# Seven products of half operands for the second layer's down projection, with the operands' sums made beside the gate and up products

## The chip, the cores and the metric

The kernel runs on one core of one Trainium2 chip. The metric is device time in microseconds (us) of one execution. A profiled execution gives the trace from which everything below is read; its times are counted from the first instruction of the span.

## The reference, cut to what matters

The program is one inference step of a two-layer trunk: an RWKV-7 layer, then a layer of band attention, each followed by a SwiGLU feed-forward part. There are 1,152 token columns (1,024 of a prompt, 128 of eight samples), 1,024 features, and 2,816 hidden features. All of it is fp32. The part at issue is the second layer's feed-forward part:

```python
def swiglu(h, w_gate, w_up, w_down):
    return (jax.nn.silu(h @ w_gate) * (h @ w_up)) @ w_down
...
        h = modulate(rms_norm(x, p['norm_ffn'][l]), sh_f, sc_f)
        x = x + gt_f[:, None, :] * swiglu(h, p['w_gate'][l], p['w_up'][l], p['w_down'][l])
```

## The kernel before, in words

Activations lie with features on the 128 partitions and tokens along the columns. The columns are held in two parts, c = 0 (512 tokens) and c = 1 (640 tokens). Every fp32 product on TensorE is made of three passes: `split` (L271) writes a rounded copy `hi` with ACT and the remainder `lo` with VectorE (DVE), and `mm3` (L275) multiplies hi by hi, hi by lo and lo by hi. So each weight tile that comes from DRAM costs one ACT and one DVE instruction, and each 128-row step of a product costs three matmuls.

**Gate and up.** `ffn` (L1392) calls `gate_up` (L1350) 22 times in the second layer, once for each f of 128 hidden features; the first of them is made in two halves. This stage already uses a Strassen-Winograd scheme: the two weight matrices against the two halves of the features, on the two halves of each token part, take seven products instead of eight. Each product is 12 matmuls of 256 columns (part 0) and 12 of 320 (part 1) into one of three PSUM tiles, S, S and PT. The products come in the order 0, 1, 2, 4, 5, 6, 3, and the names t1, s0, s1, t5, u2, u3 below are the sums into which they go. POOL (GpSimd) makes three sums of 576 columns for every f (L1369), here called ADD1 and ADD2 (into s1) and ADD3 (into t5); DVE then multiplies s1 by t5 (L1383) and s0 by u3 (L1385), and the two results go by DMA to the DRAM tensor `sd`. `strassen_weights` (L1322) loads four 128x512 weight tiles on the SP queue into the five buffers `rq`, and POOL makes four sums of them (L1340 to L1343). The weights' hi and lo lie in 16 buffers `w`, eight pairs, so weights are made about one f ahead. The token operands B fill 14 buffers of each of the two pools h0 and h1.

**Down.** The second half of `ffn` goes over 11 pairs p of hidden tiles. For each pair `begin` loads the pair of activations from `sd`, splits them, and loads four weight tiles of 128x512. For each of 8 output tiles n, part 0 takes six matmuls of 512 columns, and part 1 takes two times six of 320. DVE adds the result to the accumulators in SBUF (L1436), and at the end the residual goes in (L1170) and the result goes to `y`. Eight plain products of half operands would be the same number of columns.

**Order.** The program is written in one go and put in order by a scheduler before it runs; each engine, and the SP queue that issues nearly all DMAs, then runs its own list strictly in order. An instruction that waits holds up all that stands behind it in its list. `order` rows below show such lists.

Of the kernel before, what the change touches and what calls it, by code (L numbers as in the profile page):

```python
# [58 lines left out]
def _solver_identity():  # L59
    return np.ascontiguousarray(np.broadcast_to(np.eye(16, dtype=np.float32).reshape(1, 256), (128, 256)))  # L60
# [7 lines left out]
def _fm(v):  # L68
    return np.ascontiguousarray(np.asarray(v, np.float32).reshape(-1, 128).T)


def _tiles(w):
    k, n = w.shape
    return np.ascontiguousarray(w.reshape(k // 128, 128, n // 128, 128).transpose(2, 1, 0, 3)).reshape(n // 128, 128, k)


def prep(i):
    i = {k: np.asarray(v) for k, v in i.items()}
    d = {}
# [66 lines left out]
class Trunk:  # L146
# [372 lines left out]
    def spill(self, n, b, f, t):  # L519
        self.nc.sync.dma_start(self.sp[b][n][:, :, f, :], t.rearrange("p (w t) -> p w t", t=128))  # L520
# [753 lines left out]
    def cols(self, c):  # L1274
        return slice(512 * c, 512 + 640 * c)
# [71 lines left out]
        yield put(a21)  # L1347
        yield put(a22)

    def gate_up(self, sd, B, W, cs):  # L1350

        nc = self.nc
        dve = nc.vector
        gp = nc.gpsimd
        n0, n1 = 256 * cs[0], 576 if cs[-1] else 256
        new = (lambda: self.halfraw()[:, :n1]) if n1 == 256 else (lambda: self.ev("t")[:, n0:n1])

        def product(i):
            hi, lo = next(W)
            t = self.wide()[:, 256:832]  # L1360
            for c in cs:
                z = (t[:, 0:256], t[:, 256:576])[c]
                for k in range(4):
                    s = slice(k * 128, (k + 1) * 128)
                    self.mm3(z, hi[:, s], lo[:, s], B[c][i][0][:, k], B[c][i][1][:, k], k == 0, k == 3)
            return t[:, n0:n1]

        def add(eng, out, x, y):
            eng.tensor_tensor(out, x, y, ALU.add)  # L1369
# [6 lines left out]
        nc.scalar.activation(t5, product(4), AF.Copy)  # L1376
# [6 lines left out]
        dve.tensor_tensor(s1, s1, t5, ALU.mult)  # L1383
        add(dve, u3, product(3), u3)
        dve.tensor_tensor(s0, s0, u3, ALU.mult)  # L1385
        for h, s in enumerate((s0, s1)):
            for c in cs:
                o, n = 256 * c - n0, (256, 320)[c]
                t0 = 512 * c + n * h
                nc.sync.dma_start(sd[:, t0:t0 + n], s[:, o:o + n])  # L1390

    def ffn(self, l, B, W, part1, xsrc, dst, done):  # L1392

        nc = self.nc
        sd = [self.dp.tile([128, 2, 1152], F32, name=f"sd{l}_{p}") for p in range(11)]
        self.gate_up(sd[0][:, 0], B, iter(W), (0,))
        for _ in part1:
            pass
        self.gate_up(sd[0][:, 0], B, iter(W), (1,))
        for f in range(1, 22):  # L1400
            self.gate_up(sd[f // 2][:, f % 2], B, self.strassen_weights(l, f, nc.vector if f == 1 else None), (0, 1))
        self.ada = self.ada_steps(range(12, 28), "acc", 1) if l == 0 else iter(())
# [14 lines left out]
        for p, c in [(p, c) for p in range(9) for c in range(2)] + [(9, 1), (10, 1), (9, 0), (10, 0)]:  # L1417
# [6 lines left out]
                for n in range(8):  # L1424
                    ns = slice(n % 4 * 128, (n % 4 + 1) * 128)
                    d, parts = self.pz(c)
                    for z, o, m in parts:
                        for i in range(2):
                            wh, wl = W[p][i][n // 4]
                            hi, lo = (act[p, c][h][:, i, o:o + m] for h in range(2))  # L1430
# [12 lines left out]
                    if p == 7:  # L1443
                        x = self.ev("xin")[:, :y.shape[-1]]
# [541 lines left out]
```

## Time and profile before

| | |
|---|---|
| three runs | 3810.66 us median (3802.68 to 3817.41) |
| profiled execution, its own time | 3804.49 us |
| its span, first to last instruction | 3802.7 us |
| PE, DVE, ACT, POOL busy over the span | 92%, 60%, 41%, 16% |
| granted TensorE clock, mean | 0.940 |
| second layer's gate and up, from about 3050 us on at full clock | ends at 3520.35 us |
| second layer's down projection | 3520.35 us to the end |

In a timeline row the columns are the start, the length, the engine (SPq is the SP queue), the line, the operation, the tiles written and read, the sizes, and how many such instructions were put together; in brackets stands the idle time ahead of it and what ended it. Where rows put several matmuls together, their pace is read from the distance of two starts, since ends of matmuls are modelled and overlap. In a source row the three numbers are the shortest, the median and the longest duration in ns.

### The profile page before, as it was taken

To read this page: it belongs to the slowest core of one execution; us is meant where nothing else is said; L and a number is where in the kernel's file an instruction comes from. 1 tells how busy PE (TensorE), PEld (TensorE's weight loads), DVE (VectorE), ACT (ScalarE), POOL (GpSimd) and SP (SyncE) were. 2 spreads that over 40 slices of the span, in tenths; PEclk is the share of its full clock that TensorE was granted. 3 is DMA by queue.
4 is the path that set the end of the run, shared out by engine and by line. 5 is a ranking of instruction groups with operands and counts; after the bars stand their busy time and mean duration, and the time that the engine had idled before them with its cause. 6 is when DMAs were issued, how large, how long until landed. Compare 5 with 4: busy or idle time off the path is not lost.

```text
span 3802.7 us, 72100 instructions
## 1 busy us (share of the span) xinstructions
PE 3506.1 (92%) x28550; PEld 3098.0 (81%) x28550; DVE 2263.6 (60%) x4396; ACT 1573.8 (41%) x3006; POOL 591.6 (16%) x497
## 2 busy tenths in 40 slices
PE   5889989989999799999999899789889799999999
PEld 4777778777667699999888879667677799999898
DVE  4666667765445854554457742666565755545667
ACT  5545546544223533333311452556554533333310
POOL 0000000000011154453000100000000255444000
PEclk9887899899699899999999999899899899999999
DMA  5876776776665322224654122554565322222521
GB/s 212 236 216 170 207 220 184 201 203 201 192 197 176 113 84 76 76 73 157 221 177 172 64 71 92 153 151 155 152 203 178 120 78 71 76 75 96 171 86 66
DMA packets 426995, 554.01 MB, mean 146 GB/s; under 512 B 128385, under 2 KB 292737, under 8 KB 422177
## 3 DMA queue, kind: packets, MB, share of 16 engines
q1 hardware_dynamic: 351344, 450.68, 36.9%
q0 software_dynamic: 22224, 80.36, 6.9%
q10 hardware_dynamic: 53088, 18.36, 2.1%
q8 instruction: 225, 3.69, 0.4%
q14 instruction: 114, 0.93, 0.1%
HBM read 415.85 MB, written 133.40 MB: 144 GB/s over the span
## 4 chain that ended last, share of the span: by engine, by line
PE 69%; DMA 11%; DVE 10%; issue 4%; ACT 4%; SPq 1%; ACTq 0%; POOL 0%; DVEq 0%; POOLq 0%
PE S L143 32%; PE PT L143 15%; PE acc L143 12%; PE st L143 3%; PE O L143 2%; PE G L143 1%; DVE h L273 1%; PE aux L143 1%; PE PT L1811 1%; PE Y L143 1%; DMA TT<-Z 1%; DMA h<-out_kT 1%; DVE wlo L273 1%; DMA raw<-in_rw_o 1%; DMA h<-in_wo 1%
## 5 line engine op out<-in xcount | busy, mean ns | idle before, releaser
L143 PE MATMUL S<-h,w 128*128 128x320 f32 (+1 forms) x4944 | 689.7, 298 | 12.3 <-ACT h L272 4.8
L143 PEld LDWEIGHTS S<-h,w 128*128 128x128 f32 x4944 | 671.8, 191 | 18.4 <-ACT h L272 5.6
L143 PE MATMUL S<-h,wh 128*128 128x320 f32 (+1 forms) x2844 | 529.8, 338 | 15.9 <-DVE h L1170 6.8
L143 PE MATMUL acc<-mx,whi 128*128 128x384 f32 x1728 | 508.5, 372 | 32.7 <-ACT whi L272 13.0
L143 PEld LDWEIGHTS S<-h,wh 128*128 128x128 f32 x2844 | 456.1, 189 | 70.8 <-issue 12.3
L272 ACT ACTIVATE w<-rq 128x512 fp32r<-128x512 f32 x308 | 192.6, 629 | 515.1 <-PE S L143 201.1
L143 PEld LDWEIGHTS acc<-mx,whi 128*128 128x128 f32 x1728 | 337.6, 204 | 63.3 <-ACT whi L272 16.9
L273 DVE TENSOR_TENSOR w<-rq,w 128x512 fp32r<-128x512 f32 x308 | 267.8, 872 | 199.8 <-ACT w L272 199.0
L143 PE MATMUL PT<-h,w 128*128 128x320 f32 (+1 forms) x2448 | 347.6, 297 | 10.2 <-ACT h L272 4.7
L143 PEld LDWEIGHTS PT<-h,w 128*128 128x128 f32 x2448 | 332.1, 190 | 12.2 <-ACT h L272 5.1
L143 PE MATMUL acc<-mx,wlo 128*128 128x384 f32 x864 | 316.1, 366 | 8.3 <-DVE wlo L273 8.3
L1369 POOL TENSOR_TENSOR t<-t,t 128x576 f32<-128x576 f32 (+1 forms) x132 | 226.5, 1717 | 442.2 <-ACT t L1376 320.1
L143 PE MATMUL PT<-h,wh 128*128 128x320 f32 (+1 forms) x1428 | 284.2, 342 | 8.2 <-ACT h L1558 2.3
L143 PEld LDWEIGHTS PT<-h,wh 128*128 128x128 f32 x1428 | 231.7, 188 | 38.5 <-issue 5.0
L143 PEld LDWEIGHTS acc<-mx,wlo 128*128 128x128 f32 x864 | 175.0, 203 | 20.6 <-DVE wlo L273 12.9
L273 DVE TENSOR_TENSOR wlo<-raw,whi 128x1024 fp32r<-128x1024 f32 x114 | 139.1, 1221 | 84.9 <-ACT whi L272 83.8
L272 ACT ACTIVATE wh<-rq 128x512 fp32r<-128x512 f32 x124 | 74.8, 625 | 245.1 <-PE S L143 161.4
L273 DVE TENSOR_TENSOR h<-h,h 128x1024 fp32r<-128x1024 f32 (+4 forms) x112 | 122.3, 1106 | 88.3 <-ACT h L272 72.1
L272 ACT ACTIVATE whi<-raw 128x1024 fp32r<-128x1024 f32 x114 | 119.6, 1053 | 129.0 <-PE acc L143 62.6
L272 ACT ACTIVATE h<-h 128x1024 fp32r<-128x1024 f32 (+4 forms) x112 | 103.5, 935 | 159.8 <-DMA h<-sd 111.1
L1369 DVE TENSOR_TENSOR t<-S,t 128x576 f32<-128x576 f32 (+1 forms) x116 | 86.4, 744 | 122.7 <-PE S L143 122.7
L1436 DVE TENSOR_TENSOR h<-h,S 128x640 f32<-128x640 f32 (+1 forms) x150 | 111.9, 750 | 78.9 <-PE S L143 78.7
(444 smaller groups left out, 5625.0 us busy)
## 6 DMA issues: line engine op xcount, KB each, us to landing
h<-in_wada SPq DMA_DIRECT2D x64, 512.0 KB, 6.3
rq<-in_wg SPq DMA_DIRECT2D x88, 256.0 KB, 2.6
rq<-in_wu SPq DMA_DIRECT2D x88, 256.0 KB, 2.6
rq<-in_wd SPq DMA_DIRECT2D x88, 256.0 KB, 3.1
raw<-in_wada POOLq DMA_DIRECT2D x32, 512.0 KB, 5.0
kc<-in_ck SPq DMA_DIRECT2D x16, 1024.0 KB, 5.1
vc<-in_cv SPq DMA_DIRECT2D x16, 1024.0 KB, 6.0
sd<-t SPq DMA_DIRECT2D x88, 160.0 KB, 1.9
```

The source lines that it names most:

```text
L143: return nc.tensor.matmul(out, lhsT, rhs, start=start, stop=stop)
L272: self.nc.scalar.activation(hi, x, AF.Copy)
L273: self.nc.vector.tensor_tensor(lo, x, hi, ALU.subtract)
L1369: eng.tensor_tensor(out, x, y, ALU.add)
L1436: nc.vector.tensor_tensor(y, y, d, ALU.add)
L1811: nc.tensor.transpose(pt[:, j * 128:(j + 1) * 128], P[:, j * 128:(j + 1) * 128], self.C("ident"))
```

## The change

The second layer's down projection becomes one Strassen-Winograd scheme over the whole product: `w_down` is cut into halves of the 2,816 hidden features (even and odd tiles f) and of the 1,024 outputs, the tokens of each part into two halves. There are seven products, in the order 0, 1, 2, 4, 5, 6, 3; each has 4 output tiles m, 11 steps k of 128 hidden features, and parts of 256 and 320 columns. Both operands of the seven products need sums.

- *Activation sums* (`down_open`). After an even f its two results are held and one is stored; after an odd f DVE makes four sums of 128x576 from both pairs (t6, e1, e0, t3), and six tiles go to DRAM tensors `Bd`. The old stores to `sd` go away in this layer.
- *Weight sums* (`down_sums`). `wd1` is laid out anew by the host. It is handled in 64 groups of 88 columns: a DMA loads a 128x4x88 tile, POOL makes four sums of 128x88 in place, a DMA stores the tile to the DRAM tensors `Ws`. There is one buffer for it (`bufs=1`), so a group's load waits for the store of the group before. Three groups are written behind each f.
- *The products* (`down`). For each product, operand tiles are loaded from `Bd` and split, the weights of one m (1,408 columns) come in three loads from `Ws` or `wd1`; three products' results are held in SBUF, and DVE combines them (L1582) before the residual.

```diff
-        d[f"wd{l}"] = i["w_down"][l].reshape(22, 128, 1024)
+    d["wd0"] = i["w_down"][0].reshape(22, 128, 1024)
+    d["wd1"] = i["w_down"][1].reshape(11, 2, 128, 2, 4, 128).transpose(2, 3, 1, 4, 0, 5).reshape(128, 4, 5632)
...
         for f in range(1, 22):
-            self.gate_up(sd[f // 2][:, f % 2], B, self.strassen_weights(l, f, nc.vector if f == 1 else None), (0, 1))
+            self.gate_up(spill(f), B, self.strassen_weights(l, f, nc.vector if f == 1 else None), (0, 1))
+            if l:
+                for g in range(3 * f - 3, 64 if f == 21 else 3 * f):
+                    self.down_sums(g)
+        if l:
+            return self.down(48 * l + 40, xsrc, dst)
...
+        def odd(p):
+            def f(s0, s1, cs):
...
+                e0, e1 = held
+                t6, t3 = (self.ev("t")[:, 0:576] for _ in range(2))
+                put(p, 2, s1)
+                nc.vector.tensor_tensor(t6, s1, e1, ALU.subtract)
+                put(p, 6, t6)
+                nc.vector.tensor_tensor(e1, e1, e0, ALU.subtract)
+                put(p, 4, e1)
+                nc.vector.tensor_tensor(e0, e0, t6, ALU.add)
+                put(p, 5, e0)
+                put(p, 1, s0)
+                nc.vector.tensor_tensor(t3, s0, e0, ALU.subtract)
+                put(p, 3, t3)
...
+    def down_sums(self, g):
+
+        nc, gp = self.nc, self.nc.gpsimd
+        m, j = divmod(g, 16)
+        q = self.wq.tile([128, 4, 88], F32, tag="ws", name=self.nm("ws"), bufs=1)
+        nc.sync.dma_start(q, self.a["wd1"][:, :, g * 88:(g + 1) * 88])
+        gp.tensor_tensor(q[:, 3], q[:, 2], q[:, 3], ALU.add)
+        gp.tensor_tensor(q[:, 2], q[:, 0], q[:, 2], ALU.subtract)
+        gp.tensor_tensor(q[:, 0], q[:, 3], q[:, 0], ALU.subtract)
+        gp.tensor_tensor(q[:, 1], q[:, 1], q[:, 0], ALU.subtract)
+        nc.sync.dma_start(self.Ws[m][:, :, j * 88:(j + 1) * 88], q)
+
+    def down(self, gate, xsrc, dst):
...
+        for i in (0, 1, 2, 4, 5, 6, 3):
+            X = operand(i)
+            if i in (0, 2, 4):
+                hold(i)
+            for m in range(4):
+                W = weights(i, m)
+                d = self.wide()[:, 256:832]
+                for c in range(2):
+                    for n, (j, k) in enumerate(ks):
+                        s = slice(k * 128, (k + 1) * 128)
+                        hi, lo = (X[c][j][h][:, k] for h in range(2))
+                        self.mm3(d[:, part[c]], W[j][0][:, s], W[j][1][:, s], hi, lo, n == 0, n == 10)
...
+                if i == 1:
+                    add(oc, z, t[0])
+                    result(0, 0, m, o)
...
+                elif i == 3:
+                    add(oc, z, t[0])
+                    result(1, 0, m, o)
```

Line numbers below L133 are one higher in the changed kernel as far as L1350, so POOL's sums of L1369 and L1340 to L1343 are L1370 and L1341 to L1344 there.

POOL's list in the middle of the second layer's gate and up stage, before the change: the three sums of one f, then the four sums of weights for a later f, then ADD1 of the next f.

```order
L1369 TENSOR_TENSOR t_35036<-t_35036,t_35037 128x576 [waits DMAHW2_49,DMAHW1_49,Activation_49]
L1369 TENSOR_TENSOR t_35036<-t_35036,t_35038 128x576 [waits DVE_49,Pool_49]
L1369 TENSOR_TENSOR t_35037<-t_35037,t_35039 128x576 [waits DMAHW7_49,DMAHW0_49,DVE_49]
L1340 TENSOR_TENSOR rq_35589<-rq_35524,rq_35526 128x512 [waits DMAHW6_49,DMAHW5_49,DVE_49]
L1341 TENSOR_TENSOR rq_35524<-rq_35520,rq_35524 128x512 [waits DMAHW3_49,Pool_49]
L1342 TENSOR_TENSOR rq_35520<-rq_35589,rq_35520 128x512 [waits DVE_49,Pool_49]
L1343 TENSOR_TENSOR rq_35522<-rq_35522,rq_35520 128x512 [waits DMAHW4_49,DVE_49,Pool_49]
L1369 TENSOR_TENSOR t_35276<-t_35276,t_35277 128x576 [waits DMAHW2_49,DMAHW1_49,Activation_49]
```

The same place after the change, from ADD3 of one f on; a DMAHW wait of L1516 is that for its group's load.

```order
L1370 TENSOR_TENSOR t_33768<-t_33768,t_33770 128x576 [waits DVE_49]
L1341 TENSOR_TENSOR rq_34367<-rq_34302,rq_34304 128x512 [waits DMAHW6_49,DMAHW4_49,DVE_49]
L1342 TENSOR_TENSOR rq_34302<-rq_34298,rq_34302 128x512 [waits DMAHW0_49,Pool_49]
L1343 TENSOR_TENSOR rq_34298<-rq_34367,rq_34298 128x512 [waits DVE_49,Pool_49]
L1516 TENSOR_TENSOR ws_34547<-ws_34547 128x88 [waits DMAHW7_49,DMAHW0_49]
L1517 TENSOR_TENSOR ws_34547<-ws_34547 128x88 [waits Pool_49]
L1344 TENSOR_TENSOR rq_34300<-rq_34300,rq_34298 128x512 [waits DMAHW2_49,DVE_49]
L1518 TENSOR_TENSOR ws_34547<-ws_34547 128x88 [waits Pool_49]
L1519 TENSOR_TENSOR ws_34547<-ws_34547 128x88 [waits Pool_49]
L1516 TENSOR_TENSOR ws_34554<-ws_34554 128x88 [waits DMAHW7_49,DMAHW1_49,Pool_49]
L1517 TENSOR_TENSOR ws_34554<-ws_34554 128x88 [waits Pool_49]
L1518 TENSOR_TENSOR ws_34554<-ws_34554 128x88 [waits Pool_49]
```

Each f now has three groups in POOL's list, in this repeating order: ADD1, ADD2, group A, ADD3, three sums of weights, half of group B, the fourth sum of weights, the rest of B, group C, and then ADD1 of the next f. Groups B and C stand next to each other.

The SP queue's list at the same place before: four loads of weights, then the four stores of one f's two results.

```order
L1335 DMA rq_34080<-in_wg 128x512 [waits DMAHW3_49,DVE_49]
L1335 DMA rq_34082<-in_wg 128x512 [waits DMAHW4_49,DVE_49]
L1335 DMA rq_34084<-in_wu 128x512 [waits DMAHW5_49,DVE_49]
L1335 DMA rq_34086<-in_wu 128x512 [waits DMAHW6_49,DVE_49]
L1390 DMA sd_3_31786<-t_33596 128x256 [waits DMAHW7_49,DVE_49]
L1390 DMA sd_3_31786<-t_33596 128x320 [waits DMAHW0_49]
L1390 DMA sd_3_31786<-t_33595 128x256 [waits DMAHW1_49,DVE_49]
L1390 DMA sd_3_31786<-t_33595 128x320 [waits DMAHW2_49]
```

After, in an odd f, from the load of group B (L1515) to the store of group C (L1520):

```order
L1515 DMA ws_34547<-in_wd 128x4x88 [waits DMAHW7_49,DMAHW0_49]
L1476 DMA bd_0_31800<-t_33767 128x576 [waits DVE_49]
L1476 DMA bd_0_31812<-t_34001 128x576 [waits DMAHW2_49,DVE_49]
L1476 DMA bd_0_31797<-t_33766 128x576 [waits DVE_49]
L1476 DMA bd_0_31806<-t_33509 128x576 [waits DMAHW4_49,DVE_49]
L1476 DMA bd_0_31809<-t_33508 128x576 [waits DVE_49]
L1476 DMA bd_0_31803<-t_34002 128x576 [waits DMAHW6_49,DVE_49]
L1520 DMA ws_31816<-ws_34547 512x1x88 [waits DMAHW0_49,Pool_49]
L1336 DMA rq_34567<-in_wg 128x512 [waits DVE_49]
L1515 DMA ws_34554<-in_wd 128x4x88 [waits DMAHW7_49,DMAHW1_49]
L1336 DMA rq_34569<-in_wg 128x512 [waits DMAHW2_49,DVE_49]
L1520 DMA ws_31816<-ws_34554 512x1x88 [waits DMAHW3_49,DMAHW1_49,Pool_49]
```

The six stores of the activation sums, which wait for DVE, stand between a group's load and its store, and the loads of weights stand among the groups' loads and stores.

More of the change, by code (lines that the diff above doesn't have):

```diff
@@ L1348, in strassen_weights, with gate_up @@
         yield put(a22)
-    def gate_up(self, sd, B, W, cs):
+    def gate_up(self, put, B, W, cs):
         nc = self.nc
@@ L1385, in gate_up @@
         dve.tensor_tensor(s0, s0, u3, ALU.mult)
[L1386 to L1390, printed above, removed]
+        put(s0, s1, cs)
     def ffn(self, l, B, W, part1, xsrc, dst, done):
@@ L1395, in ffn, with spill, put @@
         sd = [self.dp.tile([128, 2, 1152], F32, name=f"sd{l}_{p}") for p in range(11)]
-        self.gate_up(sd[0][:, 0], B, iter(W), (0,))
+        def spill(f):
+            def put(s0, s1, cs):
+                for h, s in enumerate((s0, s1)):
+                    for c in cs:
+                        o, n = 256 * (c - cs[0]), (256, 320)[c]
+                        t0 = 512 * c + n * h
+                        nc.sync.dma_start(sd[f // 2][:, f % 2, t0:t0 + n], s[:, o:o + n])
+            return put
+        if l:
+            spill = self.down_open()
+        self.gate_up(spill(0), B, iter(W), (0,))
         for _ in part1:
             pass
-        self.gate_up(sd[0][:, 0], B, iter(W), (1,))
+        self.gate_up(spill(0), B, iter(W), (1,))
         for f in range(1, 22):
-            self.gate_up(sd[f // 2][:, f % 2], B, self.strassen_weights(l, f, nc.vector if f == 1 else None), (0, 1))
+            self.gate_up(spill(f), B, self.strassen_weights(l, f, nc.vector if f == 1 else None), (0, 1))
+            if l:
+                for g in range(3 * f - 3, 64 if f == 21 else 3 * f):
+                    self.down_sums(g)
+        if l:
+            return self.down(48 * l + 40, xsrc, dst)
         self.ada = self.ada_steps(range(12, 28), "acc", 1) if l == 0 else iter(())
@@ L1452, in ffn, with down_open, put, first @@
         return end
+    def down_open(self):
+        nc = self.nc
+        self.Bd = [[self.dp.tile([128, n, 576], F32, name=f"bd{i}_{j}") for j, n in enumerate((4, 4, 3))] for i in range(7)]
+        self.Ws = [self.dp.tile([128, 4, 1408], F32, name=f"ws{m}") for m in range(4)]
+        b12 = self.dp.tile([128, 576], F32, name="b12")
+        held = []
+        def put(p, i, t):
+            nc.sync.dma_start(self.Bd[i][p // 4][:, p % 4], t)
+        def first(s0, s1, cs):
+            cr = slice(256, 576) if cs[0] else slice(0, 256)
+            nc.sync.dma_start(self.Bd[0][0][:, 0, cr], s0)
+            nc.sync.dma_start(b12[:, cr], s1)
+        def even(p):
+            def f(s0, s1, cs):
+                put(p, 0, s0)
+                held[:] = s0, s1
+            return f
+        def odd(p):
+            def f(s0, s1, cs):
+                if p == 0:
+                    held[:] = (self.ev("t")[:, 0:576] for _ in range(2))
+                    nc.sync.dma_start(held[0], self.Bd[0][0][:, 0])
+                    nc.sync.dma_start(held[1], b12)
+                e0, e1 = held
[10 more added lines that the diff above has]
+                put(p, 3, t3)
+            return f
+        return lambda f: first if f == 0 else (odd if f % 2 else even)(f // 2)
@@ new lines, in down, with operand, weights, hold @@
+    def down(self, gate, xsrc, dst):
+        nc = self.nc
+        ks = [(j, k) for j, n in enumerate((4, 4, 3)) for k in range(n)]
+        part = (slice(0, 256), slice(256, 576))
+        T = {}
+        def operand(i):
+            X = {0: [], 1: []}
+            for c in range(2):
+                n = (256, 320)[c]
+                for j, nk in enumerate((4, 4, 3)):
+                    raw, hi, lo = (self.slot(c, dt)[:, :nk * n].rearrange("p (k t) -> p k t", k=nk) for dt in (F32, F32R, F32R))
+                    nc.sync.dma_start(raw, self.Bd[i][j][:, :, part[c]])
+                    self.split(hi, lo, raw)
+                    X[c].append((hi, lo))
+            return X
+        def weights(i, m):
+            src = {0: 0, 1: 1, 3: 3}.get(i)
+            src = self.Ws[m][:, {5: 0, 2: 1, 6: 2, 4: 3}[i]] if src is None else self.a["wd1"][:, src, m * 1408:(m + 1) * 1408]
+            W = []
+            for o, n in ((0, 512), (512, 512), (1024, 384)):
+                raw = self.halfraw()[:, :n]
+                nc.sync.dma_start(raw, src[:, o:o + n])
+                W.append([self.wq.tile([128, 512], F32R, tag="w", name=self.nm("w"), bufs=16) for _ in range(2)])
+                self.split(W[-1][0][:, :n], W[-1][1][:, :n], raw)
+            return W
+        def hold(n):
+            T[n] = [self.slot(c)[:, :4 * (256, 320)[c]].rearrange("p (m t) -> p m t", m=4) for c in range(2)]
+        def result(h, t, m, o):
+            f = 4 * h + m
+            at = [slice(512 * c + (256, 320)[c] * t, 512 * c + (256, 320)[c] * (t + 1)) for c in range(2)]
+            x = self.ev("xin")[:, 0:576]
+            for c in range(2):
+                nc.sync.dma_start(x[:, part[c]], xsrc[:, f, at[c]])
+            self.residual(448 if t else 576, f, gate, o, x, o)
+            for c in range(2):
+                nc.sync.dma_start(dst[:, f, at[c]], o[:, part[c]])
+        for i in (0, 1, 2, 4, 5, 6, 3):
[5 more added lines that the diff above has]
+                d = self.wide()[:, 256:832]
+                for c in range(2):
+                    for n, (j, k) in enumerate(ks):
+                        s = slice(k * 128, (k + 1) * 128)
+                        hi, lo = (X[c][j][h][:, k] for h in range(2))
+                        self.mm3(d[:, part[c]], W[j][0][:, s], W[j][1][:, s], hi, lo, n == 0, n == 10)
+                z = [d[:, part[c]] for c in range(2)]
+                t = {n: [T[n][c][:, m] for c in range(2)] for n in T}
+                o = None if i in (0, 2, 4) else self.ev("o")[:, 0:576]
+                def add(out, a, b):
+                    for c in range(2):
+                        nc.vector.tensor_tensor(out[c], a[c], b[c], ALU.add)
+                if i in (0, 2, 4):
+                    for c in range(2):
+                        nc.scalar.activation(t[i][c], z[c], AF.Copy)
+                oc = None if o is None else [o[:, part[c]] for c in range(2)]
+                if i == 1:
+                    add(oc, z, t[0])
+                    result(0, 0, m, o)
+                elif i == 4:
+                    add(t[2], t[2], t[4])
+                elif i == 5:
+                    add(t[0], z, t[0])
+                    add(oc, t[2], t[0])
+                    result(0, 1, m, o)
+                elif i == 6:
+                    add(t[0], z, t[0])
+                    add(oc, t[4], t[0])
+                    result(1, 1, m, o)
+                elif i == 3:
+                    add(oc, z, t[0])
+                    result(1, 0, m, o)
```

## The prediction

> **What bounds the kernel now.** I read the page's busy line and slices first, then the busy time by stage, then the timelines of PE and POOL in the second layer's feed-forward part, and last the sources and the DMA list for prices. Two stages matter, gate and up (to 3520.35 us) and down (from there to the end):
>
> ```profile
> PE 3506.1 (92%) x28550; PEld 3098.0 (81%) x28550; DVE 2263.6 (60%) x4396; ACT 1573.8 (41%) x3006; POOL 591.6 (16%) x497
> 3100.00:3500.00 400.00, 400.00 (x3008) 400.00 (x3007) 204.54 (x234) 128.65 (x215) 192.53 (x124) 1.00 0.22 75
> 3520.00:3802.70 282.70, 277.69 (x1588) 253.40 (x1586) 191.17 (x300) 54.19 (x73) 0.06 (x1) 1.00 0.32 106
> ```
>
> In the stage rows the columns are length, then PE, PEld, DVE, ACT and POOL busy, then the granted clock, the DMA share and GB/s. PE is busy without a gap in gate and up, and all but 5 us of the down stage, at full clock. POOL, 16% over the whole span, works 192.53 of 400 us in gate and up: the average hides that. PE sets the time in both, so its matmuls are counted from their starts:
>
> ```profile
> 3504.39 6.55 PE L143 MATMUL S<-h,w 128*128 128x256 f32 x48
> 3510.77 3.36 PE L143 MATMUL PT<-h,w 128*128 128x256 f32 x24
> 3513.97 6.55 PE L143 MATMUL S<-h,w 128*128 128x256 f32 x48
> 3520.35 1.55 PE L143 MATMUL PT<-h,wh 128*128 128x512 f32 x6
> 3528.55 1.52 PE L143 MATMUL PT<-h,wh 128*128 128x512 f32 x6
> 3533.03 1.92 PE L143 MATMUL PT<-h,wh 128*128 128x320 f32 x12
> 3543.59 1.92 PE L143 MATMUL PT<-h,wh 128*128 128x320 f32 x12
> ```
>
> From 3520.35 to 3528.55 lie 36 matmuls of 512 columns (6, 12, 6, 12): 227.8 ns each. From 3533.03 to 3543.59 lie 72 of 320: 146.7 ns. From 3504.39 to 3513.97 lie 72, half of 256 and half of 320: 133.1 ns on average, so one of 256 takes 119.4 ns. A matmul thus costs its columns plus some 13 ns.
>
> **What is removed: an eighth of the down stage's columns.** Before, 528 x 227.8 ns + 1056 x 146.7 ns = 275.2 us. After, 7 products x 4 tiles x 11 steps x 3 passes = 924 pairs of 256 and 320 columns, 924 x 266.1 ns = 245.9 us. That is 29.3 us less, where a full eighth would be 34.4: shorter matmuls give 5 back. The stage took 282.35 us: 275.2 of matmuls, 3.9 from the last matmul to the end, 3.2 of gaps. The end of it:
>
> ```profile
> 3797.29 1.52 PE L143 MATMUL S<-h,wh 128*128 128x512 f32 x6
> 3798.85 0.75 DVE L1170 SCALAR_TENSOR_TENSOR h<-S,mod,h 128x512 f32<-128x512 f32 x1 [0.61 <-PE S L143]
> L1436 DVE TENSOR_TENSOR h<-h,S 128x640 f32<-128x640 f32 x37 | 30.2, 819 | 17.3 <-PE S L143 17.3
> L1436 DVE TENSOR_TENSOR h<-h,S 128x512 f32<-128x512 f32 x38 | 25.4, 682 | 8.4 <-PE S L143 8.4
> L273 DVE TENSOR_TENSOR h<-h,h 128x1024 fp32r<-128x1024 f32 x10 | 12.2, 1225 | 19.7 <-ACT h L272 17.4 <-PE S L143 1.3 <-PE PT L143 0.9
> ```
>
> After the change two adds out of PSUM (256 and 320 columns; by the rows' slope of 1.07 ns a column 0.41 and 0.48 us) come ahead of the last residual, so the end costs about 1 us more. I leave the gaps at 3.2 us. Each product runs 35.1 us and its operands come in meanwhile. DVE, busy 68% there, gets no more work: the columns of operands to split grow from 25,344 to 44,352, 23 us at the row's 1225 ns for 1,024, but 112 accumulations of 0.68 or 0.82 us (75 of them in the rows) give way to 28 of 0.89. Bounds: gaps of nothing, or 8 us if a few products start late. So the down stage gives **28 us (23 to 31)**.
>
> **What is added on DVE and SP.** An odd f gets four sums of 128x576 on DVE, the stores of activations go from 576 KB for each f to about 1 MB, and each f gets three loads and three stores of 176 KB. By itself none of it is on PE's path: DVE is busy 51% and the DMA engines 22% there. It matters only through POOL.
>
> **What is added on POOL, and the loop it makes.** One f of gate and up lasts 22.35 us (3310.96 to 3333.31), on POOL as follows, beside DVE rows and one PE row from the same place:
>
> ```profile
> 3300.24 1.68 POOL L1342 TENSOR_TENSOR rq<-rq,rq 128x512 f32<-128x512 f32 x1 [0.69 <-DVE w L273]
> 3310.96 1.42 POOL L1369 TENSOR_TENSOR t<-t,t 128x576 f32<-128x576 f32 x1 [7.07 <-ACT t L1376]
> 3313.89 1.74 POOL L1369 TENSOR_TENSOR t<-t,t 128x576 f32<-128x576 f32 x1 [1.51 <-DVE t L1369]
> 3317.02 1.86 POOL L1369 TENSOR_TENSOR t<-t,t 128x576 f32<-128x576 f32 x1 [1.39 <-DVE t L1369]
> 3318.84 1.30 POOL L1340 TENSOR_TENSOR rq<-rq,rq 128x512 f32<-128x512 f32 x1
> 3320.21 1.69 POOL L1341 TENSOR_TENSOR rq<-rq,rq 128x512 f32<-128x512 f32 x1
> 3324.95 1.28 POOL L1343 TENSOR_TENSOR rq<-rq,rq 128x512 f32<-128x512 f32 x1 [0.68 <-DMA sd<-t]
> 3333.31 1.42 POOL L1369 TENSOR_TENSOR t<-t,t 128x576 f32<-128x576 f32 x1 [7.08 <-ACT t L1376]
> 3300.78 1.69 DVE L273 TENSOR_TENSOR w<-rq,w 128x512 fp32r<-128x512 f32 x1
> 3304.59 0.69 DVE L273 TENSOR_TENSOR w<-rq,w 128x512 fp32r<-128x512 f32 x1 [0.37 <-ACT w L272]
> 3318.91 1.83 DVE L1383 TENSOR_TENSOR t<-t,t 128x576 f32<-128x576 f32 x1 [1.32 <-POOL t L1369]
> 3320.67 0.75 DVE L1369 TENSOR_TENSOR t<-S,t 128x576 f32<-128x576 f32 x1
> 3322.37 0.74 DVE L1385 TENSOR_TENSOR t<-t,t 128x576 f32<-128x576 f32 x1
> 3319.17 3.36 PE L143 MATMUL PT<-h,w 128*128 128x256 f32 x24
> ```
>
> POOL is idle 7 us ahead of ADD1 (3310.96), then 1.5 and 1.4 us ahead of ADD2 and ADD3. Into this go three groups, and a group is more than its sums: its load waits for the store of the group before to land, and POOL, in strict order, waits for that load with everything behind it. The prices:
>
> ```profile
> L1299 POOL TENSOR_TENSOR h<-h x4: 732/848/1304, 2960.2 to 2964.1; 128x256 f32<-128x256 f32 x4
> L1341 POOL TENSOR_TENSOR rq<-rq,rq x40: 1285/1686/1688, 1338.7 to 3476.7; 128x512 f32<-128x512 f32 x40
> L469 POOL COPY shout<-hb x1: 305/305/305, 590.3 to 590.3; 128x72 f32<-128x72 f32 x1
> rq<-in_wg SPq DMA_DIRECT2D x88, 256.0 KB, 2.6
> sd<-t SPq DMA_DIRECT2D x88, 160.0 KB, 1.9
> TT<-Z ACTq DMA_DIRECT2D x36, 128.0 KB, 4.3
> ```
>
> - *A group's sums.* No row has 88 columns. From the shortest times at 256 and 512 columns (732 and 1285 ns) come 2.16 ns a column and 0.18 us fixed, an estimate of 0.37 us, and 0.07 us to the next as between 3318.84 and 3320.21: 0.44 us, 1.76 us a group. Bounds: the copy of 72 columns (0.31) and the 256-column row itself (0.73) give 1.2 to 3.2 us. I stay near the copy.
> - *A turn from one group to the next.* The store lands in 1.9 us (160 KB), the load in 2.6 (256 KB), and some 0.2 us go for the two hand-overs: 4.7 us. Bounds: 4.2 by the 128 KB store's 1.7 us and a quicker load; 6.5 if each leg moves halfway to the 4.3 us of the first layer's 128 KB DMAs.
> - *The loop.* From group A: A 1.76, ADD3 1.86 + 0.07, the four sums of weights 7.4 (3318.84 to 3326.23), B 1.76, a turn 4.7 (nothing but C stands next), C 1.76, a turn 4.7 to the next A, in which ADD1 and ADD2 run. Sum 24.0 us for an even f.
> - *Odd f.* The rows show DVE and POOL shutting each other out: a split of 0.69 us took 1.69 where it met L1342 (3300.24 to 3301.92), and L1342 took 1.68 instead of 1.29 because L1385 ran. The add out of PSUM (3320.67), inside a POOL sum, still took 0.75. The four new DVE sums all read two SBUF tiles and come just after ADD3, where POOL's sums stand; alternating them puts B's end about 1.5 us later, and B's store stands behind the six `bd` stores, the last of which waits for t3: 1.0 us more. So 26.5 us. Bounds: no addition, or 4 x 0.75 us + 2.
>
> The mean is 25.25 us against 22.35. By the Trainium skill, "SBUF — State Buffer", section "SBUF: two separate sides", the port pair of DVE and GpSimd is an exclusive lock held for a whole instruction, and the loser fully blocks. The rows above agree. By that rule alone each of the 12 short sums could meet one DVE instruction of up to 0.7 us, which would make the loop up to 30 us rather than 25.
>
> *Who waits.* DVE multiplies s1 by t5 only after ADD3, and behind that stands the add that frees product 3's PSUM tile (3320.67 to 3321.4). There are three such tiles, so PE, which began the next product at 3319.17, needs this one again two products of 3.19 us later, at 3325.6. So POOL may be 4.2 us late before PE stalls. After that PE runs at the loop's pace. The order shows three groups in each of about 18 f; the earlier groups fall in the start of the stage, where SP and POOL are idle. Cost: 18 x (25.25 - 22.35) - 4.2 = **48 us**. With loops of 22.35 and 27 us the bounds are 0 and 80 us.
>
> **The sum.** 48 - 28 = +20 us. Against the profiled execution's own 3804.5 us that is 3824.5; that execution lies 6.2 us under the median of 3810.7, so the forecast is 3810.7 + 20 = **3831 us**, slower by 0.5%.
>
> **Rivals.**
>
> 1. *The loop keeps PE's pace (faster).* Mechanism: the turns and the short sums, 9.4 and 5.3 of the 24 us. If a short sum is 0.30 us and a turn 4.2 us, the even loop is 22.2 us and the odd one, with less to collide, not far above; it decides at 22.35 us. Then only the 28 us remain: 3783 us, and with 0.5 us a round left over still under 3792. For it: POOL has 11.5 us free in each f, the groups need 5.3, and the turns could all fall in POOL's idle time. Against it: POOL's list fixes where they fall, B next to C. Chance 0.22.
> 2. *The two terms cancel (no change).* A loop of 23 to 25 us costs 8 to 44 us against 28: 3790 to 3826. For it: the sum without the odd f's additions is 24.0, which gives 25.5 us of cost, 3808 us. Against it: the collisions are in the rows already without the four new sums. Chance 0.32.
> 3. *Short pieces make DMAs slow (much slower).* A group's rows are 352 bytes. If they doubled the size-dependent part of a transfer, by the 640 and 256 KB rows about 0.9 us for 176 KB, each of the four legs in the loop would grow by that: 18 x 3.6 us = 65 us more, some 3896 us. The trace has short pieces in the first layer:
>
> ```profile
> q1 hardware_dynamic: 148715, 108.63, 43.0%
> q10 hardware_dynamic: 47680, 14.30, 7.6%
> h<-sd SPq DMA_DIRECT2D x22, 640.0 KB, 4.6
> ```
>
>  In the 860 us from 140 to 1000 us, on 16 engines, q10's packets of 300 bytes took 22 ns each, q1's of 730 bytes 40 ns: bytes count nearly in proportion. "DMA: Bandwidth & Descriptors", section "Specifications", of the Trainium skill says that under 512 bytes a transfer is a read-modify-write and falls off line rate; by it this rival would hold, and the packets above speak against it. Chance 0.04.
> 4. *The change does not save its columns.* If PE's pace were set by weight loads, 1848 loads instead of 1584 would cost. The mixed rows, 133.1 ns a matmul with a load for each, leave no room for it. It has no chance of its own.
>
> **How the numbers follow.** About 0.5%, 19 us, is what a measurement of this kernel can tell from no change. My own case, slower, has 0.42 and rival 3 0.04: slower 0.46. Rival 2: same 0.32. Rival 1: faster 0.22. The range leaves out about a tenth at each end: the lower end, 3787, takes in most of rival 1; the upper, 3868, is a loop of 27 us (80 us) with a gain of only 23 us.
>
> **What would show it.** In the changed kernel's trace: matmuls of the down stage at 119 and 147 ns, about 254 us from its first matmul to the end; f in gate and up further apart than 22.35 us; POOL's L1516 idle for DMA of `ws`, 4 to 5 us ahead of group C; PE waiting for DVE's L1370 behind L1384. The prediction is wrong if f stay 22.35 us apart, if C's load is in before B is done, or if the down stage is not near 254 us.

## The result, and the profile after

The changed kernel takes 3867.86 us (median of four runs, 3857.63 to 3879.63), the kernel before 3810.85 us on the same chip (3802.68 to 3817.41): a ratio of 1.0152 (95%: 1.0117 to 1.0187), 57 us slower. The forecast was slower by 20 us.

The profiled execution after took 3867.55 us, its span 3865.7. PE's starts divide it as they did before; the first row is the feed-forward part's first matmul, the second the down stage's:

```profile
3015.01 4.94 PE L144 MATMUL S<-h,w 128*128 128x256 f32 x24
3614.09 8.96 PE L144 MATMUL PT<-h,w 128*128 128x256 f32 x66
```

Before, the feed-forward part's first matmul was this one:

```profile
3006.39 1.95 PE L143 MATMUL S<-h,w 128*128 128x256 f32 x6 [0.67 <-ACT w L272]
```

The 8.6 us between the two starts come from stages ahead of the change; in the nine profiled executions of this study this start lies anywhere from 3006 to 3024 us. So stages are compared by their own lengths: gate and up took 513.96 us before (3006.39 to 3520.35) and takes 599.08 after, **85.1 us more**; down took 282.35 and takes 251.61 (3614.09 to 3865.7), **30.7 us less**. The sum is +54.4.

The same windows as before, after the change (length, PE, PEld, DVE, ACT, POOL busy, clock, DMA share, GB/s):

```profile
3100.00:3500.00 400.00, 361.43 (x2571) 355.74 (x2571) 207.08 (x235) 106.92 (x186) 242.09 (x289) 0.96 0.40 124
3615.00:3865.70 250.70, 245.46 (x1842) 245.20 (x1840) 134.79 (x212) 89.48 (x140) 2.62 (x2) 1.00 0.62 195
```

PE does 2571 matmuls in 400 us of gate and up instead of 3008, and it now has gaps. The down stage is nothing but matmuls. Where the gate and up stage grew is read from DVE's product of s0 and u3, once in each f. After the change the first row is that of f 1, the second that of f 20:

```profile
3101.98 0.75 DVE L1386 TENSOR_TENSOR t<-t,t 128x576 f32<-128x576 f32 x1
3597.28 0.75 DVE L1386 TENSOR_TENSOR t<-t,t 128x576 f32<-128x576 f32 x1
```

The same two before:

```profile
3078.19 1.84 DVE L1385 TENSOR_TENSOR t<-t,t 128x576 f32<-128x576 f32 x1
3499.68 0.75 DVE L1385 TENSOR_TENSOR t<-t,t 128x576 f32<-128x576 f32 x1
```

| us | before | after | difference |
|---|---|---|---|
| stage's first matmul to f 1 | 71.80 | 86.97 | +15.2 |
| f 1 to f 20, 19 f | 421.49 (22.18 each) | 495.30 (26.07 each) | +73.8 |
| f 20 to the down stage | 20.67 | 16.81 | -3.9 |

One loop on POOL, from a group A to the next (in brackets the idle time ahead of a row and what ended it). L1370 is a sum of activations, L1341 to L1344 are sums of weights, L1516 and L1519 the first and last sum of a group:

```profile
3226.40 0.38 POOL L1516 TENSOR_TENSOR ws<-ws 128x88 f32<-128x88 f32 x1 [4.53 <-DMA ws<-in_wd]
...
3228.09 1.39 POOL L1370 TENSOR_TENSOR t<-t,t 128x576 f32<-128x576 f32 x1
3229.44 1.26 POOL L1341 TENSOR_TENSOR rq<-rq,rq 128x512 f32<-128x512 f32 x1
...
3234.76 0.82 POOL L1516 TENSOR_TENSOR ws<-ws 128x88 f32<-128x88 f32 x1
...
3237.68 0.38 POOL L1519 TENSOR_TENSOR ws<-ws 128x88 f32<-128x88 f32 x1
3243.35 0.38 POOL L1516 TENSOR_TENSOR ws<-ws 128x88 f32<-128x88 f32 x1 [5.30 <-DMA ws<-in_wd]
...
3245.06 3.39 POOL L1370 TENSOR_TENSOR t<-t,t 128x576 f32<-128x576 f32 x2
3250.57 0.38 POOL L1516 TENSOR_TENSOR ws<-ws 128x88 f32<-128x88 f32 x1 [2.12 <-DMA ws<-in_wd]
```

Group B ends at 3238.06, C can start only 5.3 us later, ends at 3245.1, and the next A starts at 3250.57, although ADD1 and ADD2 (3245.06) are through at 3248.45. ADD3 (3228.09) comes behind A. In the same stretch PE waits for the add out of PSUM that stands behind it on DVE:

```profile
3232.04 5.78 PE L144 MATMUL S<-h,w 128*128 128x256 f32 x24 [4.08 <-DVE t L1370]
```

All waits of gate and up from 3060 to 3600 (us in total, times, longest), four of the rows:

```profile
ACT w L273 <- POOL rq L1344: 191.4, 20, 11.7
POOL ws L1516 <- DMA ws<-in_wd: 175.8, 40, 7.7
DVE t L1384 <- POOL t L1370: 78.8, 18, 10.1
PE S L144 <- DVE t L1370: 41.6, 18, 6.0
```

The last three are the prediction's chain, link by link: the group's load holds POOL, POOL's ADD3 holds DVE's product, and the add behind that holds PE. With 13.1 us more on PT tiles, PE's matmuls wait 54.7 us for that add in this window, and for all else 0.2. The first row, ACT waiting to split weights, is not on this path. The prices of a group, from its sums and from the DMA list between 3100 and 3550 us:

```profile
L1516 POOL TENSOR_TENSOR ws<-ws x64: 365/374/5736, 3018.6 to 3592.2; 128x88 f32<-128x88 f32 x64
ws<-in_wd SPq DMA_DIRECT2D x51, 176.0 KB, 2.9
ws<-ws SPq DMA_DIRECT2D x50, 176.0 KB, 2.4
```

### The profile page after: what moved, and what is told of

Same layout as the page of the kernel before. It is cut to its first block, busy times and chain, and to the rows that moved or that the text cites. A ratio compares the mean times of both kernels' runs of the same rounds, so it can differ in the third digit from the quotient of the medians.

```text
span 3865.7 us, 73275 instructions
## 1 busy us (share of the span) xinstructions
PE 3495.3 (90%) x28814; PEld 3105.0 (80%) x28814; DVE 2246.5 (58%) x4348; ACT 1604.2 (41%) x3074; POOL 698.4 (18%) x753
## 4 chain that ended last, share of the span: by engine, by line
PE 56%; DMA 17%; DVE 10%; issue 6%; POOL 5%; ACT 5%; SPq 1%; ACTq 0%; POOLq 0%; DVEq 0%
PE S L144 24%; PE PT L144 11%; PE acc L144 11%; DMA ws<-in_wd 3%; PE st L144 3%; DMA ws<-ws 3%; PE O L144 1%; PE G L144 1%; PE aux L144 1%; POOL ws L1516 1%; DVE h L274 1%; PE PT L1961 1%; DMA TT<-Z 1%; DMA h<-out_kT 1%; DVE wlo L274 1%
## 5 line engine op out<-in xcount | busy, mean ns | idle before, releaser
L144 PE MATMUL S<-h,w 128*128 128x256 f32 (+1 forms) x6132 | 866.6, 301 | 57.9 <-DVE t L1370 41.6
L144 PEld LDWEIGHTS S<-h,w 128*128 128x128 f32 x6132 | 843.3, 194 | 69.3 <-DVE t L1370 40.5
L273 ACT ACTIVATE w<-rq 128x512 fp32r<-128x512 f32 (+1 forms) x392 | 237.8, 618 | 594.3 <-POOL rq L1344 246.0
L274 DVE TENSOR_TENSOR w<-rq,w 128x512 fp32r<-128x512 f32 (+1 forms) x392 | 314.7, 808 | 271.8 <-ACT w L273 266.3
L144 PE MATMUL PT<-h,w 128*128 128x256 f32 (+1 forms) x3108 | 443.2, 299 | 22.8 <-DVE t L1370 13.1
L144 PEld LDWEIGHTS PT<-h,w 128*128 128x128 f32 x3108 | 426.1, 192 | 26.9 <-DVE t L1370 15.2
L144 PE MATMUL S<-h,wh 128*128 128x320 f32 (+1 forms) x1794 | 335.6, 337 | 14.8 <-DVE h L1171 5.9
L144 PEld LDWEIGHTS S<-h,wh 128*128 128x128 f32 x1794 | 285.5, 190 | 54.7 <-issue 11.9
L1370 POOL TENSOR_TENSOR t<-t,t 128x576 f32<-128x576 f32 (+1 forms) x132 | 206.8, 1568 | 247.0 <-ACT t L1377 177.1
L274 DVE TENSOR_TENSOR h<-h,h 128x1024 fp32r<-128x1024 f32 (+5 forms) x132 | 145.0, 1113 | 112.3 <-ACT h L273 100.3
L273 ACT ACTIVATE h<-h 128x1024 fp32r<-128x1024 f32 (+5 forms) x132 | 123.2, 944 | 166.4 <-DMA h<-bd 63.4
L144 PE MATMUL acc<-h,wh 128*128 128x256 f32 (+1 forms) x864 | 136.3, 306 | 17.0 <-ACT wh L273 9.0
L1370 DVE TENSOR_TENSOR t<-S,t 128x576 f32<-128x576 f32 (+1 forms) x116 | 86.2, 743 | 97.3 <-PE S L144 97.3
```

Of the source, the lines that this page charges most:

```text
L144: return nc.tensor.matmul(out, lhsT, rhs, start=start, stop=stop)
L273: self.nc.scalar.activation(hi, x, AF.Copy)
L274: self.nc.vector.tensor_tensor(lo, x, hi, ALU.subtract)
```

## The experiments

The theory: the single buffer ties each group's load to the store of the group before, and in POOL's strict list two such turns fall between one ADD3 and the next; the work itself costs nothing. The rivals: POOL's added work and its shared port with DVE; the added DMAs; DVE's four sums. Ratios are against the kernel before on the same chip. All stage lengths are read as above, each from one profiled execution; "start" is the stage's first matmul to f 1, "f" the mean of f 1 to f 20.

| kernel | ratio (95%) | gate and up | start | f | down |
|---|---|---|---|---|---|
| before | 1 | 513.96 | 71.8 | 22.18 | 282.35 |
| after | 1.0152 (1.0117 to 1.0187) | 599.08 | 87.0 | 26.07 | 251.61 |
| no sums of weights | 0.9913 (0.9884 to 0.9941) | 513.61 | 73.1 | 22.09 | 251.6 |
| no sums of activations | 1.0093 (1.0069 to 1.0117) | 585.19 | 87.5 | 25.27 | 251.6 |
| three buffers | 0.9929 (0.9904 to 0.9955) | 513.78 | 71.2 | 22.23 | 251.6 |
| one buffer, same pinning | 1.0128 (1.0098 to 1.0158) | 590.61 | 71.9 | 26.36 | 252.2 |
| two wide groups | 0.9931 (0.9909 to 0.9952) | 522.12 | 71.6 | 22.62 | 251.7 |
| no POOL sums, four an f | 1.0003 (0.9986 to 1.0021) | 545.02 | 77.4 | 23.52 | 252.0 |
| no POOL sums, three an f | 0.9910 (0.9883 to 0.9938) | 513.97 | 74.3 | 22.05 | 251.9 |

**No sums of weights.** The groups go, with their loads and stores; the products read the plain weights.

```diff
-            if l:
-                for g in range(3 * f - 3, 64 if f == 21 else 3 * f):
-                    self.down_sums(g)
...
-            src = self.Ws[m][:, {5: 0, 2: 1, 6: 2, 4: 3}[i]] if src is None else self.a["wd1"][:, src, m * 1408:(m + 1) * 1408]
+            src = {5: 0, 2: 1, 6: 2, 4: 3}[i] if src is None else src
+            src = self.a["wd1"][:, src, m * 1408:(m + 1) * 1408]
```

> No weight sums at all: no loads, no POOL sums, no stores; the seven products read plain weights, so the output isn't the reference's. DVE's four sums and the stores of activations stay. Theory: f at 22.4 to 22.8 us, 3778 to 3790 us: the down stage's gain alone. Rival 3 (DVE's four sums in every odd f and their six stores make the loop long by themselves): every second f lasts 24 us or more, 3800 to 3820 us.

Measured: 3788.46 us (3775.07 to 3793.98), ratio 0.9913. Gate and up is back at 513.6 us with all of DVE's sums and their stores in it. So the whole loss hangs on the groups, and the seven products are a gain by themselves.

**No sums of activations.** The plain tiles are stored in the sums' place; only DVE's four sums go.

```diff
-                t6, t3 = (self.ev("t")[:, 0:576] for _ in range(2))
...
-                nc.vector.tensor_tensor(t6, s1, e1, ALU.subtract)
-                put(p, 6, t6)
-                nc.vector.tensor_tensor(e1, e1, e0, ALU.subtract)
+                put(p, 6, s1)
...
-                nc.vector.tensor_tensor(e0, e0, t6, ALU.add)
...
-                nc.vector.tensor_tensor(t3, s0, e0, ALU.subtract)
-                put(p, 3, t3)
+                put(p, 3, s0)
```

> DVE's four sums of activations are left out and plain tiles are stored in their places, so the output isn't the reference's; the weight sums with their one buffer stay. Theory: all f last as the even ones do now, 24.5 to 25.3 us, and the whole is 3840 to 3855 us. Rival 3 (DVE's sums are the cause): f at 22.4 us, 3780 to 3795 us.

Measured: 3855.58 us (3848.0 to 3862.05), ratio 1.0093, 25.27 us an f. DVE's sums are worth 0.80 us an f, some 14 us of the stage: a part, not the cause.

**Three buffers, and their twin with one.** The two added buffers lie in a tile of constants that this stage no longer reads. With three buffers free the scheduler might also move the groups; so in both kernels a group's sums are pinned behind ADD3 of their own f, and as written the two differ in the buffers alone.

```diff
-        add(gp, t5, t5, u3)
+        self.pool3 = gp.tensor_tensor(t5, t5, u3, ALU.add)
...
-        q = self.wq.tile([128, 4, 88], F32, tag="ws", name=self.nm("ws"), bufs=1)
+        if g % 3:
+            q = self.cst[:, 352 * (g % 3) - 352:352 * (g % 3)].rearrange("p (a b) -> p a b", a=4)
+        else:
+            q = self.wq.tile([128, 4, 88], F32, tag="ws", name=self.nm("ws"), bufs=1)
...
+        with self.tc.issue_after(self.pool3.ins):
+            gp.tensor_tensor(q[:, 3], q[:, 2], q[:, 3], ALU.add)
...
```

> The sums of the weights keep all their work, but have three buffers in place of one (two of them in a constant tile that this stage no longer reads), and each f's three groups stand behind that f's ADD3 in POOL's list. So no sum waits for a turn of store and load. Theory (the two turns in POOL's list make the f last 26.1 us): f come back to 22.4 to 23 us, the gate and up stage to 514 to 530 us, and the whole to 3783 to 3800 us. Rival 1 (the short sums and the port that POOL shares with DVE are enough by themselves): f stay above 24.5 us, 3830 us or more. Rival 2 (DMA load or the SP queue's order, whatever POOL waits for): f stay near 26 us, about 3865 us.

Measured: 3791.24 us (3777.46 to 3796.06), ratio 0.9929. POOL in the same place (L1383 is ADD3 here, L1520 to L1523 are the sums of the three groups):

```profile
3231.34 1.93 POOL L1383 TENSOR_TENSOR t<-t,t 128x576 f32<-128x576 f32 x1 [1.33 <-DVE t L1370]
3233.23 0.38 POOL L1520 TENSOR_TENSOR ws<-ws 128x88 f32<-128x88 f32 x1
3233.56 1.23 POOL L1520 TENSOR_TENSOR cst<-cst 128x88 f32<-128x88 f32 x2
...
3242.26 0.70 POOL L1523 TENSOR_TENSOR cst<-cst 128x88 f32<-128x88 f32 x2
3242.93 1.29 POOL L1344 TENSOR_TENSOR rq<-rq,rq 128x512 f32<-128x512 f32 x1
3247.64 1.43 POOL L1370 TENSOR_TENSOR t<-t,t 128x576 f32<-128x576 f32 x1 [3.42 <-ACT t L1377]
3100.00:3500.00 400.00, 400.00 (x3010) 400.00 (x3009) 224.58 (x270) 127.95 (x216) 303.57 (x341) 1.00 0.47 143
```

All twelve short sums and the four sums of weights run from 3233.23 to 3244.22 without a wait, and POOL still has 3.4 us to spare ahead of ADD1. POOL is busier than in the changed kernel (303.57 us of 400 against 242.09), the DMA engines too (0.47 against 0.40), and PE has no gap.

> The twin of e1_three with the changed kernel's single buffer: the three groups of an f stand behind that f's ADD3 in POOL's list, as there, and only the number of buffers differs, so the turns are back in POOL's list. No group is handled before the second f. Theory: f at 25 to 27 us again. If the first groups also cost 15 us at the start of the stage, that part is gone: 1.0 to 1.3% above before, between 1.0% and 1.5% otherwise. Rival 1 (place in the list, not the turns, made e1_three fast): f at 22.4 to 23 us, 0.7% below before.

Measured for the twin with one buffer: 3862.56 us (3856.17 to 3875.44), ratio 1.0128, 26.36 us an f; its largest wait of POOL:

```profile
POOL ws L1517 <- DMA ws<-in_wd: 172.5, 39, 7.9
```

The same instructions, DMAs, bytes and pinning: the buffer alone makes 0.9929 against 1.0128. (With one buffer the scheduler spreads the groups over the f, and two turns fall between one ADD3 and the next again; with three the twelve sums stand together. That follows from the buffers.) The pair tells something else. With the groups pinned the start of the stage takes 71.9 us, as before; unpinned, in the changed kernel and in the one without sums of activations, 87.0 and 87.5. So the 15 us at the start are the early groups' doing, as far as single profiled executions show it: for the whole kernel the intervals of the twin and of the changed kernel overlap (1.0128 and 1.0152), since the twin's f are 0.3 us longer.

**Two wide groups.** One buffer again, but 44 groups of 128 columns instead of 64 of 88, two for each f: a turn less in each loop.

```diff
-                for g in range(3 * f - 3, 64 if f == 21 else 3 * f):
+                for g in range(2 * f - 2, 44 if f == 21 else 2 * f):
...
-        m, j = divmod(g, 16)
-        q = self.wq.tile([128, 4, 88], F32, tag="ws", name=self.nm("ws"), bufs=1)
-        nc.sync.dma_start(q, self.a["wd1"][:, :, g * 88:(g + 1) * 88])
+        m, j = divmod(g, 11)
+        q = self.cst[:, 0:512].rearrange("p (a b) -> p a b", a=4)
+        nc.sync.dma_start(q, self.a["wd1"][:, :, g * 128:(g + 1) * 128])
...
+        with self.tc.issue_after(self.pool3.ins):
```

> One buffer still, but 44 groups of 128 columns, two in an f, where there were 64 of 88, three in an f: the same columns and the same bytes, one turn fewer in each f, behind ADD3 as in e5_pin1. Theory: a turn of 5.5 us goes from the loop of 26.1 us, which is then under PE's 22.35 us or just above: f at 22.4 to 23.5 us, 0.2 to 0.8% below before. Rival 1 (the work of the sums): f at 25 us or more, about 1% above before.

Measured: 3792.52 us (3780.19 to 3799.57), ratio 0.9931, 22.62 us an f. POOL's wait for the load:

```profile
POOL cst L1517 <- DMA cst<-in_wd: 166.0, 42, 9.9
```

It is almost as long as the twin's 172.5 us, and yet an f is only 0.4 us longer than before, and gate and up 8 us. (The sums are also fewer, 8 instead of 12 an f at 0.46 us instead of 0.37, so this run bears out the count of turns but does not isolate it.) By this a wait in POOL's list costs little as long as the loop that it belongs to is no longer than an f.

**The DMAs without POOL's sums.** The four sums go; loads and stores stay, in the one buffer.

```diff
-        gp.tensor_tensor(q[:, 3], q[:, 2], q[:, 3], ALU.add)
-        gp.tensor_tensor(q[:, 2], q[:, 0], q[:, 2], ALU.subtract)
-        gp.tensor_tensor(q[:, 0], q[:, 3], q[:, 0], ALU.subtract)
-        gp.tensor_tensor(q[:, 1], q[:, 1], q[:, 0], ALU.subtract)
```

> The 64 groups are loaded and stored as before, through their one buffer, but POOL's four sums of each are left out, so the output isn't the reference's. SP's list and the DMA traffic stay about the same. Theory (POOL waiting in its own list for the turns is the cause): f at 22.4 to 22.8 us, 3780 to 3792 us. Rival 2 (SP's list, where the loads of weights stand among loads and stores that wait for each other, or the DMA traffic): f stay at 25 us or more, 3840 us or more.

Measured: 3819.51 us (3806.06 to 3831.89, ten runs), ratio 1.0003, neither of the expected times. Without sums the scheduler packed four groups into an f, so this run does not isolate the traffic. Its stretch of slow f (29.0, 23.1, 24.5, 24.3, 26.5, 24.1, 29.2 and 23.1 us) shows the same loop on another queue: SP's loads of a group start 5.7 us apart on average (3239.78, 3245.59, 3251.78, 3257.00), four turns are 23 us, and loads of weights stand behind them. POOL's wait for those is now the longest on its list:

```profile
POOL rq L1341 <- DMA rq<-in_wu: 107.6, 12, 14.8
```

The second version holds the groups at three an f, behind the first load of weights (`rq1`) of their f:

```diff
-                nc.sync.dma_start(q[-1], self.a[f"{n}{l}"][f][:, p * 512:(p + 1) * 512])
+                self.rq1 = nc.sync.dma_start(q[-1], self.a[f"{n}{l}"][f][:, p * 512:(p + 1) * 512])
...
+        with self.tc.issue_after(self.rq1.ins):
+            nc.sync.dma_start(q, self.a["wd1"][:, :, g * 88:(g + 1) * 88])
+            nc.sync.dma_start(self.Ws[m][:, :, j * 88:(j + 1) * 88], q)
```

> As e6_no_pool (loads and stores through the one buffer, POOL's sums of the weights left out, so the output isn't the reference's), but the scheduler may not pull the groups ahead of the f's first load of weights: three groups in an f instead of the four that it packed there. Theory: three turns of 5.5 us are 16.5 us of SP's list, so f come back to 22.4 to 22.8 us and the whole is 0.6 to 0.8% below before. Rival 2 (SP's list or the DMA traffic is enough at three groups too): f above 23.5 us, no faster than before.

Measured: 3783.26 us (3777.09 to 3784.0), ratio 0.9910, gate and up 513.97 us. Every byte that the changed kernel moves is moved here, through the same buffer, and it costs nothing that the runs can tell (0.9913 without the groups).

What the runs settle: the buffer's turn in POOL's list is the cause; POOL's work, the traffic and the port are not by themselves, since three buffers keep them all. Three buffers beat both kernels (26 us less than the kernel before on the same chip; 0.9929 against the changed kernel's 1.0152), and two wide groups reach the same ratio within the intervals with a single buffer.

## Why the prediction was right or wrong

**The down stage: right.** Forecast 254 us and a gain of 28 (23 to 31); measured 251.61 and 30.7. The first row below and the row of 3614.09 in the section on the result give 66 matmuls in 8.79 us, 133.2 ns each, as forecast (133.1):

```profile
3622.88 2.31 PE L144 MATMUL S<-h,w 128*128 128x256 f32 x18
...
3854.73 5.73 PE L144 MATMUL PT<-h,w 128*128 128x256 f32 x39
```

1848 of them are 246.1 us, and from the last (3860.46) to the end lie 5.2 us, where 4.9 were forecast. That leaves 0.3 us of gaps; the 3.2 that I left in were too many.

**The mechanism in gate and up: right; two terms of its sum were wrong.** The forecast was 48 us = 18 f x 2.9 - 4.2; measured are 85.1 = 15.2 + 19 x 3.88 - 3.9. The first step that failed is the price of a turn, 4.7 us where 5.8 were measured: two turns in each of 18 f make 39 us more, of which POOL's work, priced too dear, hid 23. The second are the early groups, put at nothing, which cost 15 us at the start of the stage. Term by term:

- *The slack of 4.2 us: right.* f 20's product is 3.9 us later against PE's matmuls than before.
- *"The earlier groups fall in the start of the stage, where SP and POOL are idle": wrong, 15 us and an f.* POOL is idle there because little is ready, but the sums of f 0 and f 1, for which PE waits, share its list with the groups. On POOL, the last groups ahead of the loop:

```profile
3057.91 5.74 POOL L1516 TENSOR_TENSOR ws<-ws 128x88 f32<-128x88 f32 x1 [5.91 <-DMA ws<-in_wd]
...
3071.46 0.37 POOL L1516 TENSOR_TENSOR ws<-ws 128x88 f32<-128x88 f32 x1 [5.36 <-DMA ws<-in_wd]
...
3072.24 0.86 POOL L1370 TENSOR_TENSOR t<-t,t 128x320 f32<-128x320 f32 x1
```

  and on PE, right behind:

```profile
3063.92 3.43 PE L144 MATMUL PT<-h,w 128*128 128x256 f32 x24
...
3076.57 5.12 PE L144 MATMUL S<-h,w 128*128 128x256 f32 x24 [6.03 <-DVE t L1370]
3081.53 3.37 PE L144 MATMUL PT<-h,w 128*128 128x256 f32 x24
```

  The sum at 3072.24 stood behind a load that came after 5.36 us, and PE lost 6.03 us to it. PE's starts divide the 15.2 us: f 1's first matmul (3063.92) comes 48.9 us after the stage's first, 44.5 before the change (3050.86) and 43.2 in the twin, so 4.4 us; the gap and the 24 matmuls behind it, 4.96 us where 24 take 3.2 at full clock, add 8.0; and f 1's product itself comes 2.8 us later behind PE, which is already part of the slack above. That the early groups cause it is shown by the pinned twin, whose start is as short as before. The same f that were thought free also run at the loop's pace: 19 f, not 18.
- *"A turn from one group to the next, 4.7 us": too short.* Over the 14 loops from 3226.40 to 3592.20 us B's end to C's start is 5.87 us on average (5.3 to 7.7) and C's end to the next A 5.69 (5.3 to 6.7). The legs are 2.4 and 2.9 us, not 1.9 and 2.6, and the hand-overs 0.4 to 0.6. Two turns make 11.6 us against 9.4. My bounds for a turn were 4.2 to 6.5. The rows I took stand for stretches in which the DMA engines were busy 0.22 of the time, and here it is 0.40. The loads of weights, 256 KB in rows of 2 KB as before, also grew from 2.5 and 2.6 us (3100 to 3500 us before) to 3.1 and 3.0 (3100 to 3550 us after), so the longer legs do not need the short pieces. That the busier DMA engines are the reason is likely, but not shown.
- *A group's sums: right.* 0.37 us each and 1.73 a group, forecast 0.37 and 1.76.
- *POOL's work and the odd f's additions: too dear, the work above all.* From ADD3's start to B's end the loop shown above, an even one, takes 9.97 us (forecast 11.1). Over the 14 loops an odd one takes 27.24 us and an even one 25.01, 2.2 more, where 2.5 was forecast; but 2.1 of it lie between A's end and B's end, where POOL's sums meet DVE's and 1.5 were forecast, and the 1.0 us for B's store behind the `bd` stores did not come as a rule, since C's turn is 5.5 to 5.7 us in five of the seven odd loops and 5.3 to 6.0 in the even ones. (Removing DVE's sums gave back less, 0.80 us an f or 1.6 for each odd one.) Work and additions together were 1.3 us an f too dear, which hid part of the turns' miss.

The mean loop comes to 26.13 us, 14.57 of work and 11.56 of turns, against a forecast of 25.25 (15.85 and 9.4). Nine tenths of a microsecond in a loop is small, but the cost is the loop's excess over f, and there 2.9 became 3.9.

**The rivals.** That the loop keeps pace needed two turns in POOL's idle time. Three turns and three groups' sums alone are 3 x (5.7 + 1.73) = 22.3 us in series, f's own length, so with one buffer nothing was left for any other wait in the list. That the two terms cancel needed a loop of 23 to 25 us; it was 26.13. Short pieces did not slow the DMAs to the forecast 3896 us, nor did weight loads set PE's pace.

**Two rules that I used.** By "SBUF — State Buffer", section "SBUF: two separate sides", of the Trainium skill the loser of the shared port blocks for the whole instruction of the other, and I gave 30 us as the loop's limit by it. Seen are a median of 374 ns for a sum that takes 365 at the least, and loops of 26.13 us: the lock is there, but most sums meet nothing. By "DMA: Bandwidth & Descriptors", section "Specifications", of the Trainium skill pieces of 352 bytes should fall off line rate; the legs took 0.3 and 0.5 us more than the rows of long pieces that I used, not the doubling of the rival, and three buffers hid even that.

## What to carry to other kernels

A buffer that is loaded, worked on in place and stored is a loop with its own length (store, load, work, times its uses for each step); put that length beside the step's, then count which turns fall between two instructions for which the critical engine waits. Work added to an idle engine is cheap, a wait added to its list is not: three buffers in place of one, or fewer and wider pieces, turned 57 us of loss into some 25 of gain here. And where an engine looks idle at the start of a stage, ask what stands in its list there before calling work free.

## What the runs showed of the hardware

**A POOL sum can be shut out through many DVE instructions.** The sum of 88 columns at 3057.91 above took 5.74 us instead of 0.37. DVE ran without a gap meanwhile; the first and last rows of that stretch:

```profile
3058.30 0.89 DVE L274 TENSOR_TENSOR h<-x,h 128x320 fp32r<-128x320 f32 x2
...
3062.51 0.90 DVE L274 TENSOR_TENSOR h<-x,h 128x320 fp32r<-128x320 f32 x2
3063.32 0.50 DVE L1370 TENSOR_TENSOR t<-PT,t 128x320 f32<-128x320 f32 x1
```

Twelve DVE instructions with two SBUF operands started in it, and the sum ended at 3063.65, when DVE read PSUM. "SBUF — State Buffer", section "SBUF: two separate sides", of the Trainium skill speaks of one whole instruction; here it was a run of them. That DVE held the sum off is read from these times alone; no run tried it apart.

**Short gaps cost PE its clock.** Ahead of 3232.04 PE was idle for 4.08 us. The window of its next 24 matmuls:

```profile
3232.00:3237.60 5.60, 5.56 (x24) 5.56 (x25) 4.02 (x4) 0.30 (x1) 4.83 (x6) 0.53 0.26 85
```

They took 5.6 us instead of 3.2 at a granted clock of 0.53; the stage's mean is 0.96 instead of 1.00. The clock is 0.50 to 0.60 over the 3.2 us behind each of the five gaps of 3.5 us and more between 3060 and 3610 us. Behind shorter ones it varies: below 2.0 us it stayed 1.00, and of the eight of 2.0 to 2.8 us three (2.06, 2.33 and 2.44 us) were followed by 1.00 and five by 0.61 to 0.69, the next one by 0.68:

```profile
3307.79 4.99 PE L144 MATMUL S<-h,w 128*128 128x256 f32 x24 [2.00 <-DVE t L1370]
```

By the POOL rows above the loop closes on POOL and its DMAs, so this should add nothing to it; that was not tried apart.
